# Output matrices of the recurrence made on Pool, thinner norm work beside the MLP, one load for the final norm, and mo in the buffers of u

## The chip, the cores and the metric

The kernel runs as one program on one core of a Trainium2 chip. The metric is device time in microseconds (us): the median over runs of the whole program. Next to it stands one profiled execution, whose trace gives the time of every instruction. The engines are PE (matrix products), DVE (elementwise work and scans), ACT (activations and copies out of the accumulators), POOL (a second elementwise engine that also issues accumulating transfers) and SP (which here only issues transfers).

## The reference, cut to what matters

One decoder layer of width 1024 over 16 meta tokens and 2048 tokens, in f32, and a final norm:

```python
hn = rms_norm(h, norm_mix_g)
b_gate, c_gate, v, u = split(hn @ w_in, [512, 1024, 1536], -1)
conv_out = b_gate * causal_dwconv(c_gate * v, conv_w)           # width 3
ssm_out  = s5_group_ssm(u, ...)   # 32 groups of 16 channels, 64 complex states each:
                                  # y = Re(C s) + D u, g = gelu(y), g * sigmoid(g @ w_glu)
mixed = concat([rms_norm(conv_out, gain_conv_out), rms_norm(ssm_out, gain_ssm_out)])
h = h + mixed @ w_out
hn = rms_norm(h, norm_ffn_g)
up = causal_dwconv(hn @ w_up, ffn_conv_w, ffn_conv_b)           # 1024 -> 2 x 2816
h = h + (silu(up[..., :2816]) * up[..., 2816:]) @ w_down
y = rms_norm(h, norm_final_g)[:, 16:]
```

`rms_norm(x, g)` is `x * rsqrt(mean(x*x) + 1e-6) * g` over the features.

## The kernel before, in words

Tokens lie along the free axis and features along the 128 partitions. The 2064 tokens are cut into six pieces of 344 (names `c0` to `c5`), or into three blocks of two pieces. Every large product is made from high and low parts (`wh_`/`wl_` of a weight, `h_`/`l_` of an activation) in three matmuls: L138, L139 and L142. ACT makes a high part (L247) and DVE the low one (L109).

The stages follow each other on PE. First come the products with `w_in`: `pu` gives u, `cv`, `cc` and `cb` the three parts of the convolution. Beside them the tables and matrices of the recurrence are made. Then the recurrence runs in eight batches of four groups (`px` in, a scan on DVE, `py` out, L806 and L807). Then the products of `w_out` with the convolution half (`pk`), the half-GLU (`pg`), the products with `w_out` (`po`), and per block of tokens the MLP: `xy` and `pz` for a tile of features, `dn` for the down product. The 22 tiles of features are in six chunks. The down product of a chunk is made in seven steps inside the next chunk, and ACT copies it out (`ev`, L1488). POOL then issues an accumulating transfer of `ev` into `h_d`, the residual stream in DRAM (L1492).

An RMS norm over a piece of tokens is a chain over all engines. `sq` are the squares, summed over tiles on DVE. `st` (L188, PE) sums over partitions, `sv` (L198, DVE) takes the mean, `sr` (L199, POOL) the power -1/2, and `dg` (L203, DVE) puts it on a diagonal. `sb` (L206, PE) spreads it over partitions, and `rs` is its copy in SBUF. Names carry what is normed: `c4` a piece of x, `mc` the convolution half, `ms` the recurrence half, `f` the MLP's input, `y` the output.

The order is that of the code. Each engine runs its own list in order, and waits where an operand or a buffer isn't ready. The norms are generators in the list `prep`. The main code calls `prep.step()` now and then, and each step runs up to `lanes` generators to their next `yield`. So the number of yields sets where in PE's, ACT's, DVE's, POOL's and SP's lists each link of a chain stands. Transfers that SP issues stand in one list too: one that waits for its buffer holds up all behind it.

Three matrices per group lie in DRAM (`mat_d`): the first is used by `px`, the other two, `mo`, by `py`. `vm` is one of them. Its eight slots take three DVE instructions each over 128x512 elements (`vm_slot`, L628): `w` twice from `bc` and `av`, and their difference. Its buffer is that of `mats`, which 32 transposes `tp` on PE (L615) still read. `ssm_load_out(b)` loads `mo` of batch b into one buffer, so that a load waits for the `py` of the batch before. `finish(b)` norms a block's output: it loads both halves of h (`sq_y`), squares them in place, and loads the same halves again as `y` to scale them.

Of the kernel before, what the change touches and what calls it, by code (L numbers as in the profile page):

```python
# [11 lines left out]
F32 = mybir.dt.float32  # L12
F32R = mybir.dt.float32r
I32 = mybir.dt.int32
AF = mybir.ActivationFunctionType
ALU = mybir.AluOpType

P = 128
D = 1024
# [3 lines left out]
NJ = 8  # L23
NC = L // NJ
# [33 lines left out]
def layer_kernel(ctx, tc, xq, pk, w_in, w_glu, w_out, w_up, w_down, ssm_s, ssm_m, y):  # L58
    nc = tc.nc
    V, S, T, G = nc.vector, nc.scalar, nc.tensor, nc.gpsimd  # L60
    dma = nc.sync.dma_start
# [13 lines left out]
    h_d = dram.tile([P, KD, L], F32, name="h_d")  # L75
    kt_d = dram.tile([15 * H * NG * H], F32, name="kt_d")
    mat_d = dram.tile([P, NG, 3, P], F32, name="mat_d")
# [20 lines left out]
    def aux_tile(name):  # L98
        return ps_ax.tile([P, 512], F32, tag="aux", name=name)
# [8 lines left out]
    def tt(out, a, b, op):  # L108
        V.tensor_tensor(out, a, b, op=op)  # L109

    def mul(out, a, b):
        tt(out, a, b, ALU.mult)
# [34 lines left out]
    def half_tile(n, name, tag="xt", bufs=3):  # L147
        return xp_.tile([P, 4, QM], F32, tag=tag, bufs=bufs, name=name)[:, :, :n]
# [32 lines left out]
    def inv_rms_of(s, nfeat, n, name, out=None, keep=False):  # L181
        sl, starts = slices(n)
        nj = len(starts)
        ps = aux_tile(f"st_{name}")
        terms = s if isinstance(s, list) else [s]
        for j, o in enumerate(starts):
            for i, a in enumerate(terms):
                T.matmul(  # L188
                    ps[:sl, j : j + 1], a[:, o : o + sl], ones[:, 0:1], start=i == 0, stop=i == len(terms) - 1
                )  # L190
        return (yield from inv_rms_at(ps[:sl, :nj], starts, nfeat, n, name, out, keep))

    def inv_rms_at(ss, starts, nfeat, n, name, out=None, keep=False):

        sl, nj = ss.shape[0], len(starts)
        v = xp_.tile([P, 8], F32, tag="sv", bufs=2, name=f"sv_{name}")
        r = xp_.tile([P, 8], F32, tag="sr", bufs=2, name=f"sr_{name}")
        V.tensor_scalar(v[:sl, :nj], ss, 1.0 / nfeat, EPS, op0=ALU.mult, op1=ALU.add)  # L198
        G.tensor_tensor(r[:sl, :nj], v[:sl, :nj], mhalf[:sl, :nj], op=ALU.pow)  # L199
        yield  # L200
        dg = xp_.tile([P, QM], F32, tag="dg", bufs=1, name=f"dg_{name}")
        for j, o in enumerate(starts):
            V.tensor_scalar(dg[:sl, o : o + sl], ident[:sl, :sl], r[:sl, j : j + 1], None, op0=ALU.mult)  # L203
        yield
        pb = aux_tile(f"sb_{name}")
        T.matmul(pb[:, :n], ones[:sl, :], dg[:sl, :n], start=True, stop=True)  # L206
        if keep:
            return pb[:, :n]
        if out is None:
            out = xp_.tile([P, QM], F32, tag="rs", bufs=2, name=f"rs_{name}")[:, :n]  # L210
        S.activation(out, pb[:, :n], AF.Copy)
        return out

    def inv_rms_from(srcs, n, name, out=None):

        ts = []
        for i, src in enumerate(srcs):
            ts.append(half_tile(n, f"sq_{name}_{i}", tag="sq", bufs=SQ))
            dma(out=ts[i], in_=src)
        yield  # L220
        yield
        if xg is not None:
            yield
            yield
        for t in ts:
            S.activation(t, t, AF.Square)
        a, b = ts
        tt(a, a, b, ALU.add)
        tt(a[:, 0:2, :], a[:, 0:2, :], a[:, 2:4, :], ALU.add)
        tt(a[:, 0, :], a[:, 0, :], a[:, 1, :], ALU.add)  # L230
        yield
        yield
        return (yield from inv_rms_of(a[:, 0, :], D, n, name, out))
# [56 lines left out]
                self.step()  # L290

    prep, ssm = Side(), Side()
    SQ = 2

    class Stream:
# [43 lines left out]
    cvp = es_a.enter_context(tc.tile_pool(name="cvp", bufs=1))  # L339
# [4 lines left out]
    a1 = None  # L344
# [55 lines left out]
    def coefficients():  # L400
# [170 lines left out]
        b1, b2, c1, c2, dd = (bc[:, i] for i in range(5))  # L571

        def over_h(a):
            return a.unsqueeze(2).to_broadcast([P, NG, H])
# [4 lines left out]
        qs, w1, w2 = (by_channel(n) for n in ("qs", "w1", "w2"))  # L579
# [46 lines left out]
        vm = a0.tile([P, NG, NJ, H], F32, tag="mats", name="vm")  # L626

        def vm_slot(i):  # L628
            mul(w1, c1, over_h(av[:, 0, i, :]))
            mul(w2, c2, over_h(av[:, 1, i, :]))  # L630
            tt(vm[:, :, i, :], w1, w2, ALU.subtract)

        for half in range(2):
            i0 = half * 4
# [69 lines left out]
    GB = 4  # L704
# [18 lines left out]

    def ssm_load_out(b):
        g0 = b * GB
        mo = a1.tile([P, GB, 2, P], F32, tag="mo", name=f"mo_{b}")
        dma(out=mo, in_=mat_d[:, g0 : g0 + GB, 1:3, :])
        mos[b] = mo

    def ssm_in(b):  # L730

# [66 lines left out]
    def ssm_out(b):  # L798
        g0 = b * GB
        mo, ub = mos[b], ld[b][1]  # L800
        gb = a1.tile([P, GB, NC], F32, tag="gb", bufs=1, name=f"gb_{b}")
        for q in range(PB):
            ps = mm_tile(f"py_{b}_{q}")
            for par in range(2):
                g = 2 * q + par
                T.matmul(ps[:, par, :NC], mo[:, g, 1, :], ub[:, g, :], start=True, stop=False)  # L806
                T.matmul(ps[:, par, :NC], mo[:, g, 0, :], yy[b][:, q, par, :], start=False, stop=True)  # L807
            S.activation(gb[:, 2 * q : 2 * q + 2, :], ps[:, :, :NC], AF.Gelu_apprx_tanh)
        S.dma_start(out=by_group(g_d)[:, g0 : g0 + GB, :], in_=gb)

# [263 lines left out]
    hos = [[] for _ in range(3)]  # L1074
    load_glu()
    prep.add(prep_glu(0, hg[0]), prep_glu(1, hg[1], **xh2))
    prep.lanes = 1
    kept = conv_part(0)
    prep.lanes = 2
    until(hg[0])  # L1080
# [258 lines left out]
    def finish(b):  # L1339
        for c in range(2):  # L1340
            s0, n = y_at(b, c)
            srcs = [h_d[:, i * 4 : i * 4 + 4, s0 : s0 + n] for i in range(2)]
            rs = yield from inv_rms_from(srcs, n, f"y{b}{c}")
            yield
            for i in range(2):
                a = half_tile(n, f"y_{b}_{c}_{i}", tag="sq", bufs=4)
                dma(out=a, in_=srcs[i])
                yield
                yield
                for k in range(4):  # L1350
                    V.scalar_tensor_tensor(
                        out=a[:, k], in0=a[:, k], scalar=col(C_FIN + 4 * i + k), in1=rs, op0=ALU.mult, op1=ALU.mult
                    )
                dma(out=y[:, i * 4 : i * 4 + 4, s0 - META : s0 - META + n], in_=a)
                yield
# [22 lines left out]
    for b in range(3):  # L1378
# [119 lines left out]
        for ci, (f0, nk) in enumerate(chunk_of):  # L1498
            if ci == last and b < 2:
                prep.drain()  # L1500
                prep.add(prep_mlp(b + 1, hf[b + 1]))
            for f in range(f0, f0 + nk):
                up(f, f == f0 + nk - 1 and ci == last)
                if f == f0 and ci:
                    for ms in first_pair:
                        down(ci - 1, ms)
                        work()
                        prep.step(2 * len(ms))
            if ci == last:
                settle()  # L1510
        if b < 2:
# [120 lines left out]
```

## Time and profile before

| | us |
|---|---|
| median of 3 runs | 2228.49 (2227.72 to 2231.98) |
| profiled execution | 2233.74 |
| its span | 2232.0 |
| PE busy | 2128.2 (95% of the span) |
| DVE busy | 1684.8 (75%) |
| ACT busy | 1101.2 (49%) |
| POOL busy | 151.9 (7%) |
| mean granted clock of PE | 0.979 of full speed |

The table gives the busy time of each engine and its share of the span. PE is busy for all but some 100 us, so a change shows where PE is idle and where its clock is granted at half, and at the places where PE would newly become idle.

### The profile page before, as it was taken

What the parts mean: (1) busy time and instruction counts of PE and PEld (TensorE: products, weight loads), DVE (VectorE), ACT (ScalarE), POOL (GpSimd) and SP (SyncE); (2) the same over time, 40 slices, a digit from 0 to 9 for tenths busy, and PEclk for the clock granted to TensorE, in tenths of its full rate; (3) what the DMA queues carried; (4) which work ended last, traced back from release to release, by engine and by line L of the source; (5) the groups of instructions that cost most, each with busy time, mean ns of one, the idle gap of its engine ahead of it and who ended that gap; (6) DMA issues with size and microseconds to landing.
All of it is one profiled execution on the core that took longest, in us unless ns stands there. A gap on an engine that the chain in (4) does not pass through costs nothing.

```text
span 2232.0 us, 33123 instructions
## 1 busy us (share of the span) xinstructions
PE 2128.2 (95%) x13012; PEld 2065.3 (93%) x13012; DVE 1684.8 (75%) x2507; ACT 1101.2 (49%) x1651; POOL 151.9 (7%) x174
## 2 busy tenths in 40 slices
PE   8997999989899999999999898999998999999997
PEld 7997999989898999999998898999998999999996
DVE  8796499848957798686768777787767879667776
ACT  4135333227523464554555555455555555555554
POOL 0000000000000001101110010100110010110000
PEclk9898999999999999999999999999999999999998
DMA  7376544352475435525554453734554463554463
GB/s 246 99 220 162 135 149 153 113 168 61 141 248 188 149 89 146 130 63 125 127 133 121 120 161 113 211 85 110 129 130 122 125 191 91 134 118 99 100 174 103
DMA packets 174909, 305.85 MB, mean 137 GB/s; under 512 B 32480, under 2 KB 108960, under 8 KB 174624
## 3 DMA queue, kind: packets, MB, share of 16 engines
q1 hardware_dynamic: 154016, 251.98, 36.5%
q0 software_dynamic: 19584, 47.52, 12.7%
q10 hardware_dynamic: 1152, 4.23, 0.5%
q8 instruction: 102, 1.67, 0.3%
q14 instruction: 55, 0.45, 0.1%
HBM read 219.86 MB, written 83.82 MB: 136 GB/s over the span
## 4 chain that ended last, share of the span: by engine, by line
PE 44%; issue 32%; DVE 11%; DMA 6%; POOL 3%; ACT 3%; SPq 0%; POOLq 0%; DVEq 0%; ACTq 0%
PE xy L1391 5%; PE xy L1393 4%; PE xy L1392 4%; PE dn L138 3%; PE dn L139 3%; PE dn L142 3%; POOL h_d L1492 3%; PE pz L1391 2%; PE pz L1393 2%; PE pz L1392 2%; PE po L138 1%; PE po L142 1%; PE po L139 1%; DMA wr_up<-in_w_up 1%; PE cc L138 1%
## 5 line engine op out<-in xcount | busy, mean ns | idle before, releaser
L109 DVE TENSOR_TENSOR wl_up<-wr_up,wh_up 128x1024 fp32r<-128x1024 f32 x198 | 241.5, 1221 | 156.0 <-ACT wh_up L247 154.0
L138 PE MATMUL dn<-ah,wh_dn 128*128 128x344 f32 (+1 forms) x1024 | 326.7, 323 | 10.4 <-ACT ah L247 8.9
L139 PE MATMUL dn<-al,wh_dn 128*128 128x344 f32 (+1 forms) x1024 | 326.0, 322 | 0.1
L247 ACT ACTIVATE wh_up<-wr_up 128x1024 fp32r<-128x1024 f32 x198 | 209.4, 1058 | 207.5 <-PE dn L139 53.9
L1391 PE MATMUL xy<-h_t,wh_up 128*128 128x344 f32 (+1 forms) x792 | 264.5, 334 | 13.3 <-ACT z L1429 7.5
L1393 PE MATMUL xy<-h_t,wl_up 128*128 128x344 f32 (+1 forms) x792 | 254.5, 321 | 0.0
L1392 PE MATMUL xy<-l_t,wh_up 128*128 128x344 f32 (+1 forms) x792 | 254.0, 321 | 0.0
L142 PE MATMUL dn<-ah,wl_dn 128*128 128x344 f32 (+1 forms) x1024 | 247.8, 321 | 0.0
L138 PEld LDWEIGHTS dn<-ah,wh_dn 128*128 128x128 f32 x1024 | 193.9, 190 | 14.8 <-ACT ah L247 9.7
L1492 POOL DMA_DIRECT2D h_d<-ev x136 | 118.3, 870 | 1271.4 <-ACT ev L1488 1266.4
L139 PEld LDWEIGHTS dn<-al,wh_dn 128*128 128x128 f32 x1024 | 194.3, 190 | 1.3 <-DVE al L109 0.8
L1391 PE MATMUL xy<-h_b,wh_up 128*128 128x344 f32 (+1 forms) x528 | 176.5, 336 | 10.6 <-ACT ev L1488 7.9
L1391 PEld LDWEIGHTS xy<-h_t,wh_up 128*128 128x128 f32 x792 | 150.2, 190 | 32.2 <-ACT z L1436 14.9
L142 PEld LDWEIGHTS dn<-ah,wl_dn 128*128 128x128 f32 x1024 | 178.5, 190 | 0.0
L1392 PE MATMUL xy<-l_b,wh_up 128*128 128x344 f32 (+1 forms) x528 | 169.5, 321 | 0.0
L1393 PE MATMUL xy<-h_b,wl_up 128*128 128x344 f32 (+1 forms) x528 | 168.3, 321 | 0.0
L1392 PEld LDWEIGHTS xy<-l_t,wh_up 128*128 128x128 f32 x792 | 150.8, 190 | 0.0
L1393 PEld LDWEIGHTS xy<-h_t,wl_up 128*128 128x128 f32 x792 | 150.7, 190 | 0.0
L247 ACT ACTIVATE wh_dn<-wr_dn 128x512 fp32r<-128x512 f32 (+1 forms) x144 | 85.5, 594 | 124.8 <-issue 43.1
L115 DVE SCALAR_TENSOR_TENSOR g<-z,pv,g 128x688 f32<-128x688 f32 (+1 forms) x132 | 122.0, 925 | 19.6 <-ACT g L1396 18.9
L109 DVE TENSOR_TENSOR wl_dn<-wr_dn,wh_dn 128x512 fp32r<-128x512 f32 (+1 forms) x144 | 92.3, 643 | 48.9 <-ACT wh_dn L247 47.8
L115 DVE SCALAR_TENSOR_TENSOR v<-z,pneg,v 128x688 f32<-128x688 f32 (+1 forms) x132 | 122.2, 926 | 9.3 <-ACT v L1396 8.1
(401 smaller groups left out, 5359.8 us busy)
## 6 DMA issues: line engine op xcount, KB each, us to landing
wr_up<-in_w_up SPq DMA_DIRECT2D x132, 512.0 KB, 5.4
h_d<-ev POOLq DMA_DIRECT2D x88, 344.0 KB, 7.1
wr_dn<-in_w_down SPq DMA_DIRECT2D x96, 256.0 KB, 2.6
wr_cw<-in_w_in SPq DMA_DIRECT2D x36, 512.0 KB, 4.4
h_d<-ev POOLq DMA_DIRECT2D x48, 336.0 KB, 6.6
x_c<-in_xq SPq DMA_DIRECT2D x16, 688.0 KB, 6.0
wr_dn<-in_w_down SPq DMA_DIRECT2D x48, 192.0 KB, 2.4
xr<-in_xq SPq DMA_DIRECT2D x24, 344.0 KB, 4.2
```

What stands on the lines that cost most here:

```text
L109: V.tensor_tensor(out, a, b, op=op)
L115: V.scalar_tensor_tensor(out=out, in0=a, scalar=s, in1=b, op0=ALU.mult, op1=ALU.add)
L138: T.matmul(ps[c], hi[:, k, :], xh, start=k == 0, stop=False)
L139: T.matmul(ps[c], hi[:, k, :], xl, start=False, stop=False)
L142: T.matmul(ps[c], lo[:, k, :], xh, start=False, stop=k == nk - 1)
L247: S.activation(hi, t, AF.Copy)
L1391: T.matmul(ps, hi[:, j, :], xh[:, j, :], start=start and j == 0, stop=False, **kw)
L1392: T.matmul(ps, hi[:, j, :], xl[:, j, :], start=False, stop=False, **kw)
L1393: T.matmul(ps, lo[:, j, :], xh[:, j, :], start=False, stop=j == 3, **kw)
L1492: G.dma_start(out=h_d[:, m, s0 : s0 + no], in_=ev, accum_op=ALU.add)
```

## The change

Five edits:

1. The 24 instructions of `vm_slot` are given to POOL instead of DVE.
2. `mo` of an odd batch is loaded by two transfers into two buffers with the tag `ut`, which held parts of u before. Only even batches use the buffer `mo`.
3. `slack` is false up to the `w_in` stage and true from `conv_part(0)` on. With it a norm has one more yield between `dg` and the matmul `sb`.
4. `inv_rms_from` always has four yields between its loads and the squares. Before, it had four only in the MLP.
5. In the MLP, `finish` loads each half of h once (`y`), squares it into another buffer (`ysq`), and scales the loaded half. `prep.step(2 * len(ms))` after a step of the down product becomes `prep.step(len(ms))`.

```diff
         yield
+        if slack:
+            yield
         pb = aux_tile(f"sb_{name}")
...
         yield
         yield
-        if xg is not None:
-            yield
-            yield
+        yield
+        yield
         for t in ts:
             S.activation(t, t, AF.Square)
...
         def vm_slot(i):
-            mul(w1, c1, over_h(av[:, 0, i, :]))
-            mul(w2, c2, over_h(av[:, 1, i, :]))
-            tt(vm[:, :, i, :], w1, w2, ALU.subtract)
+            G.tensor_tensor(w1, c1, over_h(av[:, 0, i, :]), op=ALU.mult)
+            G.tensor_tensor(w2, c2, over_h(av[:, 1, i, :]), op=ALU.mult)
+            G.tensor_tensor(vm[:, :, i, :], w1, w2, op=ALU.subtract)
...
     def ssm_load_out(b):
         g0 = b * GB
-        mo = a1.tile([P, GB, 2, P], F32, tag="mo", name=f"mo_{b}")
-        dma(out=mo, in_=mat_d[:, g0 : g0 + GB, 1:3, :])
-        mos[b] = mo
+        if b % 2 == 0:
+            mo = a1.tile([P, GB, 2, P], F32, tag="mo", name=f"mo_{b}")
+            dma(out=mo, in_=mat_d[:, g0 : g0 + GB, 1:3, :])
+            mos[b] = [mo[:, g] for g in range(GB)]
+            return
+        mos[b] = []
+        for i in range(0, GB, 2):
+            t = cvp.tile([P, NJ, 86], F32, tag="ut", bufs=2, name=f"mo_{b}_{i}").rearrange("p j x -> p (j x)")
+            mo = t[:, : 4 * P].rearrange("p (g m c) -> p g m c", g=2, m=2)
+            dma(out=mo, in_=mat_d[:, g0 + i : g0 + i + 2, 1:3, :])
+            mos[b] += [mo[:, 0], mo[:, 1]]
...
-    prep.lanes = 1
+    prep.lanes, slack = 1, True
     kept = conv_part(0)
...
     def finish(b):
         for c in range(2):
             s0, n = y_at(b, c)
-            srcs = [h_d[:, i * 4 : i * 4 + 4, s0 : s0 + n] for i in range(2)]
-            rs = yield from inv_rms_from(srcs, n, f"y{b}{c}")
-            yield
-            for i in range(2):
-                a = half_tile(n, f"y_{b}_{c}_{i}", tag="sq", bufs=4)
-                dma(out=a, in_=srcs[i])
+            xs, sq = ([half_tile(n, f"{k}_{b}_{c}_{i}", tag="sq", bufs=4) for i in range(2)] for k in ("y", "ysq"))
+            for i, a in enumerate(xs):
+                dma(out=a, in_=h_d[:, i * 4 : i * 4 + 4, s0 : s0 + n])
+            for _ in range(4):
                 yield
-                yield
+            for a, q in zip(xs, sq):
+                S.activation(q, a, AF.Square)
+            yield
...
+            rs = yield from inv_rms_of(q[:, 0, :], D, n, f"y{b}{c}")
+            yield
+            for i, a in enumerate(xs):
                 for k in range(4):
...
                         work()
-                        prep.step(2 * len(ms))
+                        prep.step(len(ms))
```

What moves can be seen in the lists of the engines, in which a line is an instruction with its output, its operands and its shape. In the `w_in` stage, this is POOL's list after the change, from the norm of piece c1 on (the name `sr_c_1494` is the power of the norm of piece c4):

```order
L199 TENSOR_TENSOR sr_c_241<-sv_c_240,mhalf 115x3
L632 TENSOR_TENSOR w_920<-bc,av 128x512
L631 TENSOR_TENSOR w_919<-bc,av 128x512
L633 TENSOR_TENSOR vm<-w_919,w_920 128x32x16
...
L633 TENSOR_TENSOR vm<-w_919,w_920 128x32x16
L199 TENSOR_TENSOR sr_c_1494<-sv_c_1493,mhalf 115x3
L631 TENSOR_TENSOR w_919<-bc,av 128x512
```

The dots stand for the rest up to the sixth slot: 18 instructions of `vm`, six slots, stand ahead of `sr_c_1494`, where before nothing stood between it and `sr_c_241`. On PE the `sb` matmul of that norm moves (its line number grows by two; rows between the two pieces that are the same in both lists are not shown):

```order
@@ -633,4 +633,5 @@
 L139 MATMUL cb_0_2_1514<-l_c1_1_213,wh_cw002_1357 128x344
 L142 MATMUL cb_0_2_1514<-h_c0_1_136,wl_cw002_1358 128x344
+L208 MATMUL sb_c4_1501<-dg_c4_1497,ones_80 128x344
 L142 MATMUL cb_0_2_1514<-h_c1_1_212,wl_cw002_1358 128x344
 L138 MATMUL cb_0_2_1514<-h_c0_1_136,wh_cw002_1357 128x344
@@ -673,5 +674,4 @@
 L139 MATMUL cv_0_3_1591<-l_c0_1_137,wh_cw083_1425 128x344
 L138 MATMUL cv_0_3_1591<-h_c1_1_212,wh_cw083_1425 128x344
-L206 MATMUL sb_c4_1501<-dg_c4_1497,ones_80 128x344
 L139 MATMUL cv_0_3_1591<-l_c1_1_213,wh_cw083_1425 128x344
 L142 MATMUL cv_0_3_1591<-h_c0_1_136,wl_cw083_1426 128x344
```

It stands 40 matmuls earlier in PE's list. At the end of the recurrence, this is SP's list before, where `mo_7` is the load for the last batch and `wr_o` are weights:

```order
L721 DMA ub_7_4185<-u_d_69 128x1032
L727 DMA mo_6_4187<-mat_d_74 128x4x256
L119 DMA wr_o004_4352<-in_w_out 128x512
L119 DMA wr_o005_4487<-in_w_out 128x512
L918 DMA mx_d_71<-tc_2_3_4319 128x2x344
L119 DMA wr_o006_4519<-in_w_out 128x512
L727 DMA mo_7_4428<-mat_d_74 128x4x256
```

And this is the same place after the change:

```order
L723 DMA ub_7_4191<-u_d_69 128x1032
L737 DMA mo_7_0_4434<-mat_d_74 128x2x256
L737 DMA mo_7_2_4436<-mat_d_74 128x2x256
L119 DMA wr_o004_4358<-in_w_out 128x512
L119 DMA wr_o005_4495<-in_w_out 128x512
L928 DMA mx_d_71<-tc_2_3_4325 128x2x344
L119 DMA wr_o006_4527<-in_w_out 128x512
```

The load for the last batch moves ahead of three loads of weights and a store. PE's list after the two `py` that open the last batch, before the change (`sb_7` is that batch's state, from DVE):

```order
L806 MATMUL py_7_0_4457<-ub_7_4185,mo_7_4428 128x258
L806 MATMUL py_7_1_4463<-ub_7_4185,mo_7_4428 128x258
L138 MATMUL pk_0_0_4482<-h_mc0_4084,wh_o000_4261 128x344
L807 MATMUL py_7_0_4457<-sb_7_4450,mo_7_4428 128x258
L806 MATMUL py_7_0_4457<-ub_7_4185,mo_7_4428 128x258
```

After the change 23 matmuls `pk` stand between those two and the first `py` that reads `sb_7`, where it was one. In the MLP this is ACT's list at the start of block 1, before the change, where `sq_y00_0` and `sq_y00_1` are the two squares of the first norm of block 0's output:

```order
L1488 ACTIVATE ev_0_5_5_11420<-dn_0_5_5_0_11389 128x672
L247 ACTIVATE wh_up1_0_1_11414<-wr_up1_0_0_11280 128x1024
L226 ACTIVATE sq_y00_0_11619<-sq_y00_0_11619 128x4x336
L247 ACTIVATE wh_up1_0_2_11452<-w4_up1_0_11380 128x512
L1488 ACTIVATE ev_0_5_6_11456<-dn_0_5_6_0_11427 128x672
...
L1488 ACTIVATE ev_0_5_7_11495<-dn_0_5_7_0_11464 128x672
L1429 ACTIVATE z_1_0_0_11498<-xy_1_0_11500 128x344
```

And after it, from the last `ev` on:

```order
L1506 ACTIVATE ev_0_5_7_11503<-dn_0_5_7_0_11472 128x672
L1447 ACTIVATE z_1_0_0_11506<-xy_1_0_11508 128x344
...
L1358 ACTIVATE ysq_0_0_0_11629<-y_0_0_0_11627 128x4x336
L1454 ACTIVATE z_1_0_1_11507<-xy_1_0_11508 128x344
L1358 ACTIVATE ysq_0_0_1_11630<-y_0_0_1_11628 128x4x336
L1456 ACTIVATE z_1_0_0_11506<-xy_1_0_11508 128x344
```

The first square has moved behind the copies `ev`, and the second is two places behind the first, where it was thirteen.

## Rows read from the trace of the kernel before

**Rows 1.** Busy time, share of the span and instructions of each engine

```profile
PE 2128.2 (95%) x13012; PEld 2065.3 (93%) x13012; DVE 1684.8 (75%) x2507; ACT 1101.2 (49%) x1651; POOL 151.9 (7%) x174
```

**Rows 2.** Stretches: length, busy PE PEld DVE ACT POOL (x), clock, DMA

```profile
118.00:163.00 45.00, 45.00 (x289) 44.67 (x288) 42.36 (x72) 19.25 (x25) 1.16 (x1) 1.00 0.79 216
163.00:218.00 55.00, 40.38 (x228) 36.88 (x227) 39.31 (x61) 25.14 (x22) 2.90 (x3) 0.88 0.68 173
...
470.00:482.00 12.00, 5.22 (x16) 4.01 (x15) 8.28 (x15) 0.70 (x2) 0.00 (x0) 0.72 0.60 197
...
536.00:612.00 76.00, 65.40 (x376) 61.80 (x375) 67.34 (x100) 41.01 (x42) 6.10 (x6) 0.93 0.35 109
...
1198.00:1260.00 62.00, 50.90 (x291) 49.32 (x290) 40.49 (x45) 31.43 (x47) 6.92 (x8) 0.92 0.61 164
...
1340.00:1352.00 12.00, 4.92 (x21) 4.64 (x20) 3.70 (x4) 4.75 (x8) 0.86 (x1) 0.73 0.58 176
...
1698.00:1750.00 52.00, 44.14 (x252) 42.55 (x252) 33.53 (x37) 26.11 (x35) 6.92 (x8) 0.93 0.72 188
```

**Rows 3.** Waits of PE: line, awaited, us in total, times, longest

```profile
PE xy L1391 <- ACT ev L1488: 7.9, 2, 4.1
PE xy L1391 <- ACT z L1429: 7.5, 2, 7.1
PE py L806 <- DMA mo<-mat_d: 6.8, 1, 6.8
PE sb_mc L206 <- DVE dg_mc L203: 4.6, 3, 3.8
```

**Rows 4.** Groups of DVE, 121.3 to 141.2 us: busy, mean ns | idle before

```profile
L109 DVE TENSOR_TENSOR w<-bc,av 128x512 f32<-128x512 f32 x14 | 9.0, 680 | 0.0
L109 DVE TENSOR_TENSOR vm<-w,w 128x512 f32<-128x512 f32 x8 | 5.4, 679 | 0.0
```

**Rows 5.** The tile mats: instructions with ns min/median/max, first and last start

```profile
L615 PE MATMUL tp<-ident,mats x32: 270/272/454, 95.5 to 120.9; 128*128 128x128 f32 x32
```

**Rows 6.** Groups of POOL over the span: busy, mean ns | idle before

```profile
L199 POOL TENSOR_TENSOR sr_c<-sv_c,mhalf 115x3 f32<-115x3 f32 x8 | 8.8, 1105 | 325.3 <-DVE sv_c L198 325.3
...
masks.py:199 POOL TENSOR_SCALAR_AFFINE_SELECT ident<-ident 128x128 f32<-128x128 f32 x1 | 0.3, 293 | 0.1
```

**Rows 7.** Timeline of POOL: start us, us, instruction [idle before <-releaser]

```profile
20.49 2.23 POOL L199 TENSOR_TENSOR sr_c<-sv_c,mhalf 115x3 f32<-115x3 f32 x1 [19.18 <-DVE sv_c L198]
...
187.36 0.85 POOL L199 TENSOR_TENSOR sr_c<-sv_c,mhalf 115x3 f32<-115x3 f32 x1 [18.38 <-DVE sv_c L198]
```

**Rows 8.** Timeline of DVE at three places

```profile
20.53 1.22 DVE L109 TENSOR_TENSOR wl_u<-wr_u,wh_u 128x1024 fp32r<-128x1024 f32 x1
...
476.24 0.69 DVE L109 TENSOR_TENSOR sb<-zi,zr 64x514 f32<-64x514 f32 x1
...
1315.27 0.66 DVE L203 TENSOR_SCALAR dg_y<-ident,sr_y 112x112 f32<-112x112 f32 x3 [0.84 <-POOL sr_y L199]
```

**Rows 9.** Timeline of PE at three places

```profile
139.67 0.74 PE L206 MATMUL sb_c<-dg_c,ones 115*128 115x344 f32 x2
...
166.68 0.76 PE L188 MATMUL st_c<-ones,sq_c 128*115 128x1 f32 x6 [3.33 <-DVE sq_c L109]
...
477.98 2.06 PE L806 MATMUL py<-ub,mo 128*128 128x258 f32 x4 [6.78 <-DMA mo<-mat_d]
```

**Rows 10.** Timeline of SP: issues of transfers

```profile
471.23 0.38 SPq L727 DMA_DIRECT2D mo<-mat_d  x1
...
1238.92 0.38 SPq L219 DMA_DIRECT2D sq_y<-h_d  x1
```

**Rows 11.** Timeline of ACT at the start of block 1

```profile
1227.09 1.32 ACT L226 ACTIVATE sq_y<-sq_y 128x1344 f32<-128x1344 f32 x1 [6.32 <-DMA sq_y<-h_d]
...
1237.12 0.46 ACT L1436 ACTIVATE z<-xy 128x344 f32<-128x344 f32 x1 [0.56 <-PE xy L1393]
...
1243.05 1.33 ACT L226 ACTIVATE sq_y<-sq_y 128x1344 f32<-128x1344 f32 x1 [1.92 <-DMA sq_y<-h_d]
```

More of the change, by code (lines that the diff above doesn't have):

```diff
@@ L292, in layer_kernel @@
     prep, ssm = Side(), Side()
+    slack = False
     SQ = 2
@@ L805, in ssm_out @@
                 g = 2 * q + par
-                T.matmul(ps[:, par, :NC], mo[:, g, 1, :], ub[:, g, :], start=True, stop=False)
-                T.matmul(ps[:, par, :NC], mo[:, g, 0, :], yy[b][:, q, par, :], start=False, stop=True)
+                T.matmul(ps[:, par, :NC], mo[g][:, 1, :], ub[:, g, :], start=True, stop=False)
+                T.matmul(ps[:, par, :NC], mo[g][:, 0, :], yy[b][:, q, par, :], start=False, stop=True)
             S.activation(gb[:, 2 * q : 2 * q + 2, :], ps[:, :, :NC], AF.Gelu_apprx_tanh)
@@ L1341, in finish @@
             s0, n = y_at(b, c)
-            srcs = [h_d[:, i * 4 : i * 4 + 4, s0 : s0 + n] for i in range(2)]
-            rs = yield from inv_rms_from(srcs, n, f"y{b}{c}")
-            yield
-            for i in range(2):
-                a = half_tile(n, f"y_{b}_{c}_{i}", tag="sq", bufs=4)
-                dma(out=a, in_=srcs[i])
-                yield
-                yield
+            xs, sq = ([half_tile(n, f"{k}_{b}_{c}_{i}", tag="sq", bufs=4) for i in range(2)] for k in ("y", "ysq"))
[5 more added lines that the diff above has]
+                S.activation(q, a, AF.Square)
+            yield
+            q = sq[0]
+            tt(q, q, sq[1], ALU.add)
+            tt(q[:, 0:2, :], q[:, 0:2, :], q[:, 2:4, :], ALU.add)
+            tt(q[:, 0, :], q[:, 0, :], q[:, 1, :], ALU.add)
+            yield
+            rs = yield from inv_rms_of(q[:, 0, :], D, n, f"y{b}{c}")
+            yield
+            for i, a in enumerate(xs):
                 for k in range(4):
```

## The prediction, made before the result was known

> **What bounds the kernel now.** I read the busy times first [rows 1]: PE works for 2128.2 of the span's 2232.0 us, so nearly all of the time is matmuls that the change leaves as they are. What can be won or lost is PE's idle time (about 104 us) and the stretches where its clock is granted at 1.2 instead of 2.4 GHz. Next the stretches [rows 2]: the reader is to see that PE's idle time lies in a few places. From 118 to 163 us it is busy for all 45.00 us at clock 1.00; right after, it is idle for 14.6 of 55. From 470 to 482 it works 5.22 of 12 us at a mean clock of 0.72, thus 2 x 0.28 x 12 = 6.7 us at the lower level. Further holes lie at 536 to 612 (10.6 us idle), 1198 to 1260 (11.1), 1340 to 1352 (7.1) and 1698 to 1750 (7.9). Third, the waits of PE [rows 3] say who ended these: the load of `mo` (6.8), the `dg` of a norm (3.8 of 4.6), and ACT, which copies out `ev` or `z` late (two of about 4, one of 7.1). Each edit aims at one such place. Last the timelines of POOL, DVE, SP and ACT, for the prices.
>
> After each long idle time the clock is low for a while: besides the wait of 6.78 us there are the 7.1 at 1341, with (1 - 0.73) x 2 x 12 = 6.5 us low. About 6.6 us at half speed after a long stall cost up to 3.3 us of work; I use that below.
>
> **Edit 1, vm on POOL.** DVE gives up 24 instructions. The 22 of them in one window took 9.0 + 5.4 = 14.4 us [rows 4], back to back with idle 0.0. PE had no idle time in that stretch, so this gain by itself is worth nothing there; it can only bring the next norm's squares earlier, for which PE waited 3.33 us at 166.68 [rows 9].
>
> The price is POOL's order: 18 instructions now stand ahead of `sr_c_1494`, and PE reaches the matmul behind that power 40 matmuls earlier than before. At 45.00/289 = 0.156 us a matmul, that is 139.67 - 6.2 = 133.4 us [rows 2, 9]. The first slot's two `w` can go early, but `vm` takes the buffer of `mats`, which `tp` reads until 120.9 [rows 5]. So 16 instructions are left from 121 us. No row shows POOL at a two-input instruction of 512 elements. Bounds: as fast as DVE, 0.68 us [rows 4]; from POOL's own elementwise instruction of 128 elements, 4 x 0.293 = 1.17 [rows 6]; and slower if it is held up by DVE as `sr_c` is. That took 0.85 alone (187.36), 1.105 in the mean of eight, and 2.23 when DVE's two-input `wl_u` of 1.22 us ran beside it [rows 6 to 8]; adding that excess of 1.38 gives 2.55. I take 1.17 and the mean excess of 0.25: 1.4 us.
>
> 16 x 1.4 = 22.4, so POOL is through at 143.4. Then the power with 1.1 and three `dg` with 0.66 [rows 8]: 145.2. PE stands from 133.4: 11.8 us, and 3.3 for the low clock after it. Of this the 3.33 us before `st_c` come back, since DVE and ACT run on during the stall and DVE has less to do; the two waits after it hang on links behind `st_c` and stay. Net 11.8 + 3.3 - 3.3 = **+11.8**. At 0.68 POOL is through at 131.9 and PE stands for hardly half a us: about -3. At 1.17 it is +8. At 2.55 it is 161.8, and +30.
>
> The profile first: `sr_c` is long only with DVE beside it, 2.23 against 0.85 us [rows 7, 8]. The Trainium skill, page "SBUF — State Buffer", section "Who interferes with whom", gives a reason: an instruction of DVE with two SBUF inputs and one of GpSimd that reads SBUF exclude each other, and the second waits for all of the first. By that rule a POOL instruction between DVE's long ones would come near the upper price, and the sum would be that of the second rival below. Of the price alone, the Trainium skill, page "GPSIMD Engine Reference", section "Elementwise — side-by-side cycle accounting", gives 4497 ns for 2048 elements; a quarter of it, as an estimate, is 1.12 us, next to the 1.17 above.
>
> **Edit 2, mo in the buffers of u.** In SP's list the last load of `mo` stood behind weights and a store and went out at 471.23 [rows 10]; PE waited 6.78 us for it, to 477.98 [rows 9]. Now it is issued with `ub`, ahead of all of these, and has landed by then. What is late next is the state `sb` of the last batch: its second half of the first pair starts on DVE at 476.24 and takes 0.69 [rows 8], so 476.9. PE comes to it at 471.2 plus the two `py` (2.06 us at the low clock, so 1.0) and the 23 `pk` that now stand between, 3.6: 475.8. So 1.1 of 6.78 us stay. Of the clock: if the 6.7 low us of the stretch lie at its end, the four from 477.98 to 482 ran at half speed, 2 us of loss, which go. **-7.7**, with bounds 0 (another load or DVE is as late) and -9. Four more issues on SP at 0.38 us [rows 10] lie where SP waits for buffers anyway.
>
> **Edits 3 and 4, yields in the norms.** A yield later the `sb` of the half-GLU and of the output norms finds its `dg` done; the wait of 3.8 us goes and most of the 0.8 left in that row [rows 3]. But a chain with one more yield is finished later, and its consumers are due at the same time: part of it turns up before `st` or before the products. I take a third of that row's 4.6 us: **-1.5**. Bounds: all of the stretch's 10.6 us idle [rows 2], or as much in the other direction as one long wait, +4.
>
> **Edit 5, the MLP.** Eight loads of h go; they run on the DMA queues beside PE, so they are worth nothing unless somebody waits. At 1227.09 ACT had waited 6.32 us for the first square's load with the copies `ev` behind it [rows 11], and PE for these. The square now stands behind the copies, so that wait, 4.1 us in each of two blocks, goes. What is late next: the second square is two places behind the first, but the buffer for its load comes free no sooner. That load went out at 1238.92 and its square began at 1243.05 [rows 10, 11]. ACT is now there at about 1237, when it made the last `z` [rows 11], and stands 6 us, with PE's next `z` behind it. So PE's three short stalls there become one of about 6. The holes of 11.1 and 7.9 us stay within 2 us of what they were. The hole of 7.1 at 1341 hung on loads and stores of this norm; with half as many steps per matmul it is spread, I take half of it, -3.5. More steps of the chains fall late in the block: +1 to +2 for a later square of the next norm. Sum **-2.5**, bounds -12 (all three holes without their first two us and half of the low clock) and +8 (a second stall of 6 us in each of two blocks, less what goes).
>
> **Sum.** 11.8 - 7.7 - 1.5 - 2.5 = +0.1 us on an execution of 2233.74, which lies 5.25 above the median of the runs, 2228.49. So 2228.6, rounded 2229, for the median: no change that can be told. A measurement of this kernel can tell about 0.2%, 4.5 us, from none.
>
> **Rivals.**
> *Faster: POOL is quick enough, or PE has little to wait for.* At 0.9 us an instruction POOL is through at 135.3, PE's stall is 3.7 us, about what returns, and up to 3.3 for the clock: +0 to +4 instead of +11.8, and the sum is -12 to -8: 2219. For it: DVE runs the same at 0.68, and it has 14 us less to do, so that less stands in POOL's way. Against it: 0.293 us for 128 elements, and `sr_c` with three elements takes 0.85.
> *Slower: POOL and DVE exclude each other.* At 1.9 us an instruction, POOL is through at 151.4 and PE's stall is 19.8: +19.8, and the sum +8.1: 2237. It decides from 1.7 us on, where the sum passes 4.5. For it: 2.23 beside `wl_u`, and DVE was busy for 42.36 of 45 us there [rows 2]. Against it: without `vm` it is busy for some 28, and the mean excess is only 0.25.
> *Slower: the second square.* ACT's wait for it comes on top of the first hole instead of in its place, 6 us in each of two blocks, against -2.5: +12 and 2240 at its full price; half of it is likelier, 2234. For it: ACT's order is fixed, and `z` stands behind the square. Against it: the same load was waited for before.
> *The change at `mo` does nothing.* If `sb` comes later by as much as PE comes earlier, -7.7 is -1: 2235. Against it: 23 matmuls stand between.
>
> **How the numbers follow.** No change 0.38; faster 0.34; slower by POOL 0.16, by the square 0.08, by `mo` 0.04. So faster by over 0.2% 0.34, within 0.38, slower 0.28. The forecast's own range is 2224 to 2233. For 8 in 10 the range goes to the rivals: 2215 to 2241.
>
> **What would show it.** Edit 1: `vm` on POOL from 121 us at about 1.4 us each, `sr_c` beginning near 143, and a wait of PE for `dg_c` of about 12 us at the `sb` of piece c4 with the clock low after it. Edit 2: no wait for `mo`; at most 1 to 2 us for `sb`. Edits 3 and 4: no wait of PE for `dg_mc` over 2 us. Edit 5: ACT waits about 6 us for `ysq`'s second load at the start of blocks 1 and 2, not for the first, and the hole at 1341 is about half. If `vm` takes under 1 us, or PE's wait for `dg_c` is under 5 us, the forecast is wrong to the fast side; if `vm` takes 1.7 us or more, to the slow side.

## The result, and the profile after

The changed kernel takes 2240.76 us (median of 6 runs, 2236.5 to 2248.74), the one before 2228.78 in the same comparison. The ratio is 1.0052, with a 95% interval of 1.0042 to 1.0063: slower by 12 us. The profiled execution took 2239.21 us, with a span of 2237.4.

The busy times after, answering to [rows 1]:

```profile
PE 2128.1 (95%) x13012; PEld 2066.7 (92%) x13012; DVE 1676.1 (75%) x2483; ACT 1102.4 (49%) x1651; POOL 182.9 (8%) x198
```

PE has the same work. DVE lost 24 instructions but only 8.7 us, where they alone had taken 14.4 us and more [rows 4]: what is left on DVE got longer. The stretches around the `w_in` stage after the change (length, then busy time of PE, PEld, DVE, ACT and POOL, clock, share of DMA, GB/s), against 118 to 218 us in [rows 2]:

```profile
118.00:137.80 19.80, 18.26 (x118) 17.43 (x117) 13.32 (x31) 7.25 (x13) 12.26 (x9) 1.00 0.59 146
137.80:153.30 15.50, 0.00 (x0) 0.00 (x0) 5.82 (x6) 0.00 (x0) 14.95 (x14) 0.57 0.33 110
153.30:175.00 21.70, 21.66 (x124) 21.22 (x125) 11.42 (x16) 6.76 (x9) 2.11 (x2) 0.91 0.81 217
```

In the second row nothing works but POOL and a little DVE. PE's timeline shows what it waited for, here and at the other places of the prediction:

```profile
153.34 1.49 PE L208 MATMUL sb_c<-dg_c,ones 115*128 115x344 f32 x2 [15.57 <-DVE dg_c L203]
188.99 1.51 PE L208 MATMUL sb_c<-dg_c,ones 115*128 115x344 f32 x2 [3.18 <-DVE dg_c L203]
...
496.90 0.70 PE L817 MATMUL py<-sb,mo 128*128 128x258 f32 x2 [1.19 <-DVE sb L109]
...
585.80 1.29 PE L188 MATMUL st_mc<-ones,sq_mc 128*115 128x1 f32 x6 [4.93 <-DVE sq_mc L109]
...
1251.90 0.66 PE L1409 MATMUL xy<-h_b,wh_up 128*128 128x344 f32 x1 [5.23 <-ACT z L1456]
1352.43 0.65 PE L1409 MATMUL xy<-h_t,wh_up 128*128 128x344 f32 x1 [2.78 <-ACT z L1454]
1443.46 0.42 PE L1409 MATMUL xy<-h_t,wh_up 128*128 128x344 f32 x1 [4.66 <-ACT z L1447]
```

The 3.33 us before `st_c` [rows 9] are gone, and the 6.78 for `mo` became 1.19 for `sb`. The 3.8 for `dg_mc` [rows 3] became 4.93 for `sq_mc`: PE now waits at `st_mc`, its matmul before `sb_mc` in the chain of the norm. In the MLP, the wait of 7.1 us that ended near 1348 [rows 3] became one of 2.78, and a new one of 4.66 stands near 1443. The start of block 1 has one wait of 5.23 us.

POOL's timeline after shows part of the queue ahead of the power, and what follows it:

```profile
125.14 1.59 POOL L633 TENSOR_TENSOR vm<-w,w 128x512 f32<-128x512 f32 x1 [25.49 <-PE tp L617]
126.81 1.92 POOL L631 TENSOR_TENSOR w<-bc,av 128x512 f32<-128x512 f32 x1
128.70 1.06 POOL L632 TENSOR_TENSOR w<-bc,av 128x512 f32<-128x512 f32 x1
...
145.38 1.26 POOL L633 TENSOR_TENSOR vm<-w,w 128x512 f32<-128x512 f32 x1
146.60 0.85 POOL L199 TENSOR_TENSOR sr_c<-sv_c,mhalf 115x3 f32<-115x3 f32 x1
147.42 1.06 POOL L631 TENSOR_TENSOR w<-bc,av 128x512 f32<-128x512 f32 x1
...
149.57 1.77 POOL L633 TENSOR_TENSOR vm<-w,w 128x512 f32<-128x512 f32 x1
151.42 1.70 POOL L631 TENSOR_TENSOR w<-bc,av 128x512 f32<-128x512 f32 x1
```

The reader is to see 16 instructions from 125.14 to 146.60, 1.34 us each, and two kinds of durations: 1.06 (`w`) or 1.26 to 1.31 (`vm`) where DVE stands still, up to 1.92 where it works. And DVE's timeline beside it:

```profile
125.50 2.32 DVE L109 TENSOR_TENSOR wl_cw<-wr_cw,wh_cw 128x1024 fp32r<-128x1024 f32 x1
...
147.48 1.07 DVE L203 TENSOR_SCALAR dg_c<-ident,sr_c 115x115 f32<-115x115 f32 x1 [10.07 <-POOL sr_c L199]
148.47 1.75 DVE L115 SCALAR_TENSOR_TENSOR tc<-cvt,pv,tc 128x688 f32<-128x688 f32 x1
150.14 1.27 DVE L203 TENSOR_SCALAR dg_c<-ident,sr_c 115x115 f32<-115x115 f32 x1
151.34 0.86 DVE L109 TENSOR_TENSOR tc<-tc,rs 128x688 f32<-128x688 f32 x1
152.12 1.07 DVE L203 TENSOR_SCALAR dg_c<-ident,sr_c 115x115 f32<-115x115 f32 x1
...
155.35 2.04 DVE L241 SCALAR_TENSOR_TENSOR t_c<-x_c,pv,rs_c 128x344 f32<-128x344 f32 x4 [1.20 <-ACT rs_c L213]
```

The same instructions before, with POOL idle:

```profile
126.32 1.21 DVE L109 TENSOR_TENSOR wl_cw<-wr_cw,wh_cw 128x1024 fp32r<-128x1024 f32 x1
...
132.83 0.92 DVE L115 SCALAR_TENSOR_TENSOR tc<-cvt,pv,tc 128x688 f32<-128x688 f32 x1
...
136.27 0.27 DVE L203 TENSOR_SCALAR dg_c<-ident,sr_c 115x115 f32<-115x115 f32 x1
```

`wl_cw` takes 2.32 instead of 1.21 us, and a `dg` 1.07 to 1.27 instead of 0.27. Each of the three `dg` ends 0.07 us after the POOL instruction that was at work when it began (at 148.48, 151.34 and 153.12), so DVE was held until POOL was through. The three `dg` and the two `tc` between them took from 147.48 to 153.19, 5.7 us. In front of them DVE itself stood still for 10.07 us, waiting for POOL.

PE was late before it came to that `sb`. POOL's first `w`, at 83.02 us, ran beside DVE's `w`, for which the matmuls `kps` wait. Before and after:

```profile
83.33 0.47 DVE L596 TENSOR_SCALAR w<-bc,pv 128x512 f32<-128x512 f32 x1
...
83.70 1.29 DVE L598 TENSOR_SCALAR w<-bc,pv 128x512 f32<-128x512 f32 x1
```

PE's wait at `kps` rose from 0.92 to 1.75 us, and from 100 to 110 us its clock was granted at 0.87, before at 1.00. PE came to the place of `sb` at 137.8 us, where before it passed that place at 133.3. The other kernels with all of `vm` on POOL were there at 137.4 (e2) and 136.8 (e4), those with none of it on POOL between 131.9 and 135.1.

In the MLP, ACT's first `ysq` does not wait, and the second does, with the copy `z` behind it for which PE waits at 1251.90:

```profile
1241.53 1.32 ACT L1358 ACTIVATE ysq<-y 128x1344 f32<-128x1344 f32 x1
1242.75 0.44 ACT L1454 ACTIVATE z<-xy 128x344 f32<-128x344 f32 x1
1250.18 1.32 ACT L1358 ACTIVATE ysq<-y 128x1344 f32<-128x1344 f32 x1 [6.99 <-DMA y<-h_d]
1251.41 0.44 ACT L1456 ACTIVATE z<-xy 128x344 f32<-128x344 f32 x1
```

To compare the runs by stage, I take five matmuls that end a wait in every trace: the `cb` after a wait of 0.8 us for `cvt` (at 286.2 us before), the first `xy`, and the first `dn` of the last group of each block. Each column is the time from one to the next (us, from one profiled execution each):

| kernel | w_in | to first xy | block 0 | block 1 | block 2 | tail |
|---|---|---|---|---|---|---|
| before | 286.2 | 466.6 | 449.8 | 499.9 | 475.2 | 54.2 |
| after | 306.1 | 461.1 | 446.1 | 495.8 | 476.2 | 52.2 |
| e1 no POOL | 290.6 | 458.9 | 446.1 | 496.1 | 478.5 | 52.1 |
| e2 POOL only | 306.4 | 467.0 | 448.9 | 498.8 | 475.7 | 53.3 |
| e3 MLP only | 288.7 | 467.9 | 446.4 | 503.1 | 472.5 | 54.1 |
| e4 no power | 300.6 | 459.3 | 447.8 | 495.7 | 474.5 | 52.6 |
| f1 mo, yields | 287.2 | 461.2 | 446.5 | 509.7 | 481.7 | 51.9 |
| f2 mo only | 285.1 | 462.7 | 449.2 | 498.7 | 478.0 | 54.4 |
| f3 yields only | 285.4 | 464.2 | 447.1 | 506.3 | 480.8 | 52.0 |
| f4 old steps | 286.6 | 461.2 | 449.4 | 492.6 | 478.9 | 51.8 |
| g1 old steps, off | 287.1 | 458.8 | 449.9 | 493.8 | 481.9 | 54.8 |
| g2 mo, yields, off | 287.2 | 461.3 | 448.4 | 497.7 | 477.0 | 54.7 |
| g3 two on POOL | 289.8 | 458.0 | 447.6 | 497.1 | 475.4 | 52.1 |
| g4 off | 284.9 | 461.1 | 446.5 | 505.5 | 476.2 | 53.9 |

"Off" is `slack` set back to false where the MLP starts. The changed kernel loses 19.9 us in the first column and gains 14.5 in the others. Without POOL the first column scatters from 284.9 to 290.6. The profiled execution of before took 2233.74, 5 us above its median, and that of after 1.5 below: the spans differ by 5.4 us, the medians by 12. For sizes I therefore use the ratios, and the table for the place.

### The profile page after: what moved, and what is told of

It is laid out like the page before. It is cut to its first block, busy times and chain, and to the rows that moved or that the text cites. A ratio compares the mean times of both kernels' runs of the same rounds, so it can differ in the third digit from the quotient of the medians.

```text
span 2237.4 us, 33123 instructions
## 1 busy us (share of the span) xinstructions
PE 2128.1 (95%) x13012; PEld 2066.7 (92%) x13012; DVE 1676.1 (75%) x2483; ACT 1102.4 (49%) x1651; POOL 182.9 (8%) x198
## 5 line engine op out<-in xcount | busy, mean ns | idle before, releaser
L248 ACT ACTIVATE wh_dn<-wr_dn 128x512 fp32r<-128x512 f32 (+1 forms) x144 | 85.6, 594 | 133.3 <-issue 52.5
```

The costliest lines, as they stand in the source:

```text
L248: S.activation(hi, t, AF.Copy)
```

## The experiments

Each ratio is to the kernel before on the same chip, with its 95% interval, from 5 rounds.

**e1: all but POOL.** The changed kernel with `vm_slot` as before.

```diff
-            G.tensor_tensor(w1, c1, over_h(av[:, 0, i, :]), op=ALU.mult)
+            mul(w1, c1, over_h(av[:, 0, i, :]))
```
(and the two lines below it alike)

> The changed kernel with the 24 instructions of vm back on DVE, all other edits kept. Theory (POOL's queue costs, the rest gains): the wait of 15.6 us at the sb of piece c4 is gone and sb stands where it stood before; by 236 us the changed kernel was 19.9 us behind the one before, and from there to the end it gained 14.5. So 2221 us (2217 to 2225), 0.3% under before. Rival (the MLP edit is what costs, the stall at c4 is mostly returned later): 2234 or more. Rival (edits 2 to 5 gain only by filling PE's time after the stall): near 2229.

Measured: 2224.04 against 2232.52, 0.9964 (0.9952 to 0.9977). The theory is right and the rivals fall: without edit 1 the change is faster by 8 us. Against 1.0052 with it, edit 1 costs 0.0088, 20 us.

**e2: POOL alone.** The kernel before with only this:

```diff
-            mul(w1, c1, over_h(av[:, 0, i, :]))
+            G.tensor_tensor(w1, c1, over_h(av[:, 0, i, :]), op=ALU.mult)
```
(and the two lines below it alike)

> The kernel before with vm on POOL and nothing else changed. Theory: +14 to +20 us at piece c4, nothing returned later except the 3.3 us before st_c, which are in that sum: 2245 us (2241 to 2249). Rival (the stall is mostly returned later): 2230 to 2234. Rival (the MLP edit costs): 2229.

Measured: 2248.43 against 2232.52, 1.0077 (1.0065 to 1.0089), +17 us. The theory is right and both rivals fall. PE waits 15.57 us at the same `sb`. In the five stretches after it 2 us in all come back. The `sb` stands at its earlier place here too, 13 matmuls ahead of `cv_0_3`, as in the changed kernel; in e1 and in every other run without `vm` on POOL it stands 27 matmuls behind the first of `cv_0_3`, as before. So it is edit 1, and not the yields, that moves it by 40 matmuls: the lists don't follow the order of the code alone, but depend too on the engine that an instruction is given to.

**e3: the MLP alone.** The kernel before with the new `finish` and

```diff
-                        prep.step(2 * len(ms))
+                        prep.step(len(ms))
```

> The kernel before with only the edits in the MLP (finish loads h once, half as many steps of the norms beside down). Theory: in the two traces the stretches from 753 to 1203, 1203 to 1703 and 1703 to 2177 us changed by -3.7, -4.1 and +0.9 us, so -4 to -7: 2223 us (2220 to 2227). Rival (the second square's wait of 7.0 us on ACT in two blocks is a loss): 2232 to 2238.

Measured: 2235.12 against 2232.52, 1.0014 (1.0006 to 1.0023): a loss of 3 us, nearer to the rival. Block 0 takes 3.3 us less, block 1 3.2 more, and PE has a new hole of 7.43 us near 1429. I had taken the gain from a trace in which other edits were at work as well.

**e4: the queue apart from the rest.** The changed kernel, with the power of one piece left out and a copy on DVE in its place.

```diff
-        G.tensor_tensor(r[:sl, :nj], v[:sl, :nj], mhalf[:sl, :nj], op=ALU.pow)
+        if name == "c4":
+            V.tensor_copy(r[:sl, :nj], v[:sl, :nj])
+        else:
+            G.tensor_tensor(r[:sl, :nj], v[:sl, :nj], mhalf[:sl, :nj], op=ALU.pow)
```

> The changed kernel, but for piece c4 alone the power -1/2 on POOL is replaced by a copy on DVE (the power is left out there, so the output is not the layer's). vm stays on POOL with its 24 instructions. It tells POOL's queue from POOL and DVE slowing each other. Theory (queue): PE's wait at the sb of piece c4 falls from 15.6 to under 4 us and the time to 2225 us (2221 to 2229). Rival (DVE is slowed so much by POOL that the dg are as late anyway): the wait stays above 8 us, 2234 or more.

Measured: 2239.07 against 2232.52, 1.0027 (1.0017 to 1.0037). Neither fits whole. PE's wait did fall:

```profile
142.32 1.49 PE L211 MATMUL sb_c<-dg_c,ones 115*128 115x344 f32 x2 [5.52 <-DVE dg_c L206]
```

But the time is at the rival's. Without any of POOL's work it is 0.9964. So 0.0063, 14 us, stay though nothing of this norm waits in POOL's queue for `vm`, and taking the power out of it gives back 0.0025, 5.6 us. The trace is of the fastest of nine runs, 2232.36 us, so it shows places and not the size. It has DVE slow while POOL goes on. The next link of the chain, eight `t_c`, in this run:

```profile
144.34 4.69 DVE L244 SCALAR_TENSOR_TENSOR t_c<-x_c,pv,rs_c 128x344 f32<-128x344 f32 x4 [2.16 <-ACT rs_c L216]
148.95 0.86 DVE L109 TENSOR_TENSOR tc<-cb,tc 128x688 f32<-128x688 f32 x1
149.73 4.71 DVE L244 SCALAR_TENSOR_TENSOR t_c<-x_c,pv,rs_c 128x344 f32<-128x344 f32 x4
```

and in the kernel before:

```profile
141.23 3.98 DVE L240 SCALAR_TENSOR_TENSOR t_c<-x_c,pv,rs_c 128x344 f32<-128x344 f32 x8
```

1.17 us each instead of 0.50, 5.4 us more for the eight. PE then waits in three places for `h_c`, `l_c` and `tc`, in all 5.2 us.

But these slow `t_c` are e4's own: in the changed kernel they come when POOL is nearly through, and the first four take 2.04 us (at 155.35 above), as before. So e4 shows that a loss of 14 us is there without the queue; it doesn't divide the changed kernel's 20 us between queue and exclusion. A third cause is in both and was not tested: `sb` at its earlier place, which PE reached at 136.8 us here and at 140.3 in e1. At the old place, some 6 us of matmuls later, PE would have found the `dg` of e4 done. No run has `vm` on POOL and `sb` where it stood before.

**f1: mo and the yields.** The changed kernel with `vm_slot`, `finish` and the steps of the MLP as before; of the diff these remain:

```diff
+            t = cvp.tile([P, NJ, 86], F32, tag="ut", bufs=2, name=f"mo_{b}_{i}").rearrange("p j x -> p (j x)")
...
+    prep.lanes, slack = 1, True
```

> The changed kernel without the edits on POOL and in the MLP: mo in the buffers of u and the yields in the norms remain. Theory (the edits add up; the MLP edit is a small loss, 1.0014 alone): the changed kernel with vm back on DVE had 0.9964 of the time before, so 0.995 of before (0.994 to 0.996). Rival (with one more yield per norm the halved steps in the MLP are needed, and the MLP edit gains there): 0.998.

Measured: 2238.85 against 2229.26, 1.0038 (1.0023 to 1.0053). Both fall: this is a loss of 8 us, and the edit of the MLP that costs 3 us alone is worth 16 beside these (1.0038 to 0.9964).

**f2: mo alone.** The kernel before with

```diff
+            t = cvp.tile([P, NJ, 86], F32, tag="ut", bufs=2, name=f"mo_{b}_{i}").rearrange("p j x -> p (j x)")
```
(and the lines around it)

> The kernel before with only mo of odd batches in the buffers of u. Theory: the load's wait of 6.8 us falls to 1.2 and 2 us of low clock go: -7.7 us, 0.9965 of before (0.9955 to 0.9975). Rival (a later wait in the glu products takes some of it, 2.2 us for wl_g in the trace after): -4 to -5, 0.998.

Measured: 2229.86 against 2229.26, 1.0003 (0.9993 to 1.0012): no change that can be told, so theory and rival both fall. In its trace the wait for `mo` is gone:

```profile
475.89 0.70 PE L815 MATMUL py<-sb,mo 128*128 128x258 f32 x2 [1.19 <-DVE sb L109]
...
508.37 0.65 PE L142 MATMUL pg<-gh,wl_g 128*128 128x344 f32 x1 [2.34 <-DVE wl_g L109]
```

and the stretch to the first `xy` is 3.9 us shorter. Of the 5.6 us, 0.65 go to the new wait for `wl_g`, which stands in place of one of 1.69 for `wl_o` before. Nor is the low clock gone: it comes after that wait. The same two places, before and in f2 (columns as above):

```profile
471.00:482.00 11.00, 4.22 (x11) 3.31 (x11) 7.28 (x13) 0.60 (x1) 0.00 (x0) 0.69 0.57 184
510.00:545.00 35.00, 31.52 (x197) 30.91 (x196) 32.32 (x31) 26.92 (x27) 1.67 (x2) 0.98 0.27 79
...
471.00:482.00 11.00, 9.81 (x56) 8.99 (x56) 6.87 (x12) 1.83 (x3) 0.00 (x0) 1.00 0.53 164
505.00:540.00 35.00, 30.64 (x173) 29.92 (x172) 32.58 (x31) 26.14 (x26) 1.96 (x2) 0.89 0.26 76
```

In the two places together 6.8 + 1.4 = 8.2 us were at the lower level before, and 7.7 in f2. That the medians show none of the 3.9 us isn't explained by these traces; block 2 took 2.8 us more in this one.

**f3: the yields alone.** Edits 3 and 4 in the kernel before:

```diff
+        if slack:
+            yield
...
+    prep.lanes, slack = 1, True
```

> The kernel before with only the yields: one more ahead of sb from conv_part(0) on, four ahead of the squares. Theory (what is left when mo has its -7.7): -3 us, 0.9985 of before (0.998 to 0.9995). Rival (the waits only move from dg_mc to sq_mc and sq_ms): 1.000.

Measured: 2241.03 against 2229.26, 1.0052 (1.0038 to 1.0065): a loss of 12 us, and both theory and rival fall. Between the `cb` and the first `xy` it gains 2.4 us. Block 1 takes 6.4 and block 2 5.6 us longer, where PE has two new holes:

```profile
1429.27 0.66 PE L138 MATMUL dn<-ah,wh_dn 128*128 128x344 f32 x1 [7.35 <-ACT ev L1490]
...
1848.61 0.66 PE L1393 MATMUL xy<-h_b,wh_up 128*128 128x344 f32 x1 [4.96 <-ACT z L1440]
```

ACT's timeline says why the first came. A square of the next block's norm stands ahead of a copy `ev` and waits for its load. At the second, ACT had waited 7.15 us with weights, `wr_up`, next in its list; why is not shown:

```profile
1415.03 0.73 ACT L1490 ACTIVATE ev<-dn 128x688 f32<-128x688 f32 x1
1426.30 1.35 ACT L227 ACTIVATE sq_f<-sq_f 128x1376 f32<-128x1376 f32 x1 [10.54 <-DMA sq_f<-h_d]
1427.55 1.04 ACT L248 ACTIVATE wh_up<-wr_up 128x1024 fp32r<-128x1024 f32 x1
1428.50 0.72 ACT L1490 ACTIVATE ev<-dn 128x688 f32<-128x688 f32 x1
...
1847.15 1.06 ACT L248 ACTIVATE wh_up<-wr_up 128x1024 fp32r<-128x1024 f32 x1 [7.15 <-DVE wr_up L109]
```

**f4: the old number of steps.** e1 with one line as before.

```diff
-                        prep.step(len(ms))
+                        prep.step(2 * len(ms))
```

> The changed kernel with vm back on DVE and the old number of steps beside the down product (2 per matrix tile), so that finish with one load per half of h remains of the MLP edit. Theory (the halved steps push the next norm's squares into the copies ev, a hole of 7.2 us at 1418 that the kernel before does not have): 0.994 to 0.9955 of before. Rival (finish itself costs, by the second square's wait of about 5 us in two blocks): 0.997 or more, no better than with the halved steps.

Measured: 2221.45 against 2229.26, 0.9967 (0.9955 to 0.9979). Not to be told from e1's 0.9964, so the theory isn't borne out. Against f1's 1.0038 the new `finish` alone is worth 16 us: it, and not the halved steps, is what the yields need. Block 1 is shorter by 3.5 us and block 0 longer by 3.3: the hole near 1418 is gone, and others have come.

**g1 to g4.** Three set `slack` back where the MLP starts:

```diff
     prep.drain()
+    slack = False
```

g1 is f4 with it, g2 is f1 with it, g4 is e1 with it. g3 is the changed kernel with slots 6 and 7 of `vm` on POOL and the others on DVE:

```diff
+            e = G if i >= 6 else V
-            G.tensor_tensor(w1, c1, over_h(av[:, 0, i, :]), op=ALU.mult)
+            e.tensor_tensor(w1, c1, over_h(av[:, 0, i, :]), op=ALU.mult)
```

> The changed kernel with vm back on DVE, the old number of steps in the MLP, and slack set back to false where the MLP starts. Theory (the extra yield inside the MLP costs: in all traces with it the stretch of block 2 is 450 to 453 us, without it 445 to 449, and the tail gives back 2): 3 to 4 us less than with slack on (0.9967), so 0.995 of before (0.9942 to 0.996). Rival (beside finish with one load the extra yield does no harm): 0.9965 or more.

Measured: 2224.39 against 2233.43, 0.9960 (0.9947 to 0.9973). With slack on it was 0.9967, so theory and rival aren't told apart.

> The kernel before with mo in the buffers of u and the yields in the norms, but slack set back to false where the MLP starts, and the MLP as before. With slack on in the MLP it was 1.0038. Theory (the loss of the yields is all in the MLP): 0.9975 of before (0.996 to 0.999). Rival (the yields cost ahead of the MLP): 1.002 or more.

Measured: 2227.72 against 2233.43, 0.9970 (0.9960 to 0.9980). The theory is right: f1's 1.0038 falls by 0.0068, 15 us, by the line `slack = False`. Blocks 1 and 2 are 12.0 and 4.7 us shorter.

> The changed kernel with only the last two of the eight slots of vm on POOL; these six instructions stand behind the power of piece c4 in POOL's list. With all of them on DVE it was 0.9964, with all on POOL 1.0052. Theory (queue and exclusion both scale with the POOL instructions at work while DVE is on the path): 0.997 to 0.9985, the wait at the sb of c4 under 1 us. Rival (any POOL work there stretches the next chain on DVE as in the run without the power): 1.000 or more.

Measured: 2223.88 against 2233.43, 0.9960 (0.9947 to 0.9973). The rival falls, and the theory was too high. The wait at the `sb` of c4 is gone, and the six instructions cost nothing that can be measured against e1. Here `sb` stands 21 matmuls behind the first of `cv_0_3`, near its old place. They collide with DVE all the same:

```profile
140.82 2.29 POOL L634 TENSOR_TENSOR vm<-w,w 128x512 f32<-128x512 f32 x1
143.19 1.92 POOL L632 TENSOR_TENSOR w<-bc,av 128x512 f32<-128x512 f32 x1
```

> The changed kernel with vm back on DVE and slack set back to false where the MLP starts, halved steps kept. With slack on it was 0.9964. Theory (the MLP edit needs the extra yield, since alone it was 1.0014): 0.998 (0.997 to 0.9995). Rival (the extra yield costs whatever else is done): 0.995 or less.

Measured: 2229.78 against 2233.43, 0.9979 (0.9969 to 0.9988). The theory is right: with slack on it was 0.9964. In the table block 1 takes 505.5 us here and 503.1 in e3 (the MLP edit without the yield), 506.3 and 509.7 in f3 and f1 (the yield without the edit), and 496.1 with both, 499.9 and 497.7 with neither.

Six versions beat both kernels: g1 and g3 (0.9960), e1 (0.9964), f4 (0.9967), g2 (0.9970) and g4 (0.9979). Their intervals overlap, so no best one is named.

## Why the prediction was right or wrong

The range, 2215 to 2241, held 2240.76 barely. The likeliest case, no change, did not come: it is the slower side, to which I had given 0.28.

**The step that failed is the sum of edit 1,** +11.8 us, where the comparisons give 17 (e2) to 20 (e1). Its first half came as forecast. POOL's instruction took 1.34 us for 1.4, and PE waited at the `sb` of c4. POOL began at 125 instead of 121 us, since `tp` ended later. PE came later by as much, which leaves the stall as it was but is itself a loss of some 4 us that I had put at nothing. Of the next links I had taken three `dg` at 0.66 in sum; they took 5.7 with the `tc` between them, held up by POOL. With the stall of 15.57, the 4 us before it, 2 for the low clock and the 3.33 that came back the sum is about 18. I had priced the exclusion on POOL's side alone, as 0.25 us on each of its instructions. It falls on both, and e4 shows that 14 us are lost even when nothing of this norm waits in POOL's queue. How the changed kernel's 20 us divide among the queue, the exclusion and the earlier place of `sb` stays open.

**The rival that POOL and DVE exclude each other** was right in its mechanism and near in its sum (+8.1, measured +12), and wrong in its price: I had set it to decide from 1.7 us an instruction of POOL on, and it decided at 1.34, by what it did to DVE. That its +19.8 for edit 1 lies within the measured 17 to 20 is luck. Here the trace agrees with the Trainium skill, page "SBUF — State Buffer", section "Who interferes with whom": whoever comes second waits for the whole of the other. The page also counts `copy` and `tensor_scalar` among those that can contend, and the trace has them: `dg` at 1.07 for 0.27, and the copy `halo`, of 128x2 elements, at 0.74 for 0.16.

**Edit 2.** The wait came out as forecast, 1.19 us for `sb` where I had 1.1. The term of -7.7 is not in the time: f2 measures 1.0003, between -1.6 and +2.7 us. Some 3.9 us are seen in the trace. What I left out is that the low clock doesn't go with the wait: it comes again after the new wait for `wl_g`, so hardly any of the 2 us I had counted for it are there.

**Edits 3 and 4,** -1.5 us. I looked only at the stages ahead of the MLP, where f3's trace has -2.4, and forgot that `slack` stays true in the MLP. Alone the yields are +12 us (f3), and g2 shows that this loss is made in the MLP. For one of the two new holes of PE the trace shows the cause: a square has moved ahead of a copy on ACT.

**Edit 5,** -2.5 us. At the start of the blocks it went as forecast: no wait for the first square, 6.99 us on ACT for the second (I had 6), and 5.23 on PE. The hole at 1341 fell from 7.1 to 2.78 us, more than the half I had taken, but the 4.66 near 1443 are new. In the sum the edit has no one size. It is +3 us alone (e3), about +2 (g2 to g4) without the extra yield, and -16 with it (f1 to e1). Edits 3 and 5 move the same squares. In block 1, ACT waits for the load of a square `sq_f` once for long before, 10.32 us near 1345; twice with either edit alone (7.82 and 8.82 in e3, 10.70 and 10.54 in f3); and once with both (7.82 in e1).

So the remainder of the change was forecast at -11.7 and measured at -8 (e1). That it is near in sum is luck, for none of its parts has the size that I gave it. Why g2 is at 0.9970 while mo alone is at 1.0003 is open: the yields ahead of the MLP would have to be worth 7 us, where the traces show 2.

## What to carry to other kernels

Work moved to an idle engine is not free for the engine it came from, if the two hold each other up as DVE and POOL do here: price each instruction of both engines that runs beside the other, the small ones of a dependent chain first. Before moving long work into an engine's list, look for short links of a critical chain behind it, and read the lists of the other engines again: here a matmul of PE moved with it. Two edits that move the same waits have to be measured together, and a flag set for one stage is to be followed to the end of the program.

## What the runs showed of the hardware that was not expected

Small DVE instructions suffer most in proportion: beside POOL's two-input work, a 115x115 TENSOR_SCALAR went from 0.27 to 1.07 and 1.27 us, and a 128x344 SCALAR_TENSOR_TENSOR from 0.50 to 1.17 (e4). POOL's own instruction took 1.06 us (`w`) or 1.26 to 1.31 (`vm`) undisturbed and up to 2.29 (g3).

After the wait of 15.57 us the clock was granted at 0.91 in the mean over the next 21.7 us: 2 x 0.09 x 21.7 = 3.9 us at the lower level, about 2 us of loss, where I had taken 3.3.
